# Twelve 2 KB buffers for nine, transposition chains begun at the end of their product, x split by halves of a chunk, and the first MLP product done two blocks at a time

## The chip, the cores and the metric

The kernel runs on one core of a Trainium2 chip. The metric is the device time of one execution in microseconds (us). The engines are TensorE (PE, matrix products, with its weight loads shown apart as PEld), VectorE (DVE), ScalarE (ACT), GpSimdE (POOL) and SyncE (SP), which here issues all transfers. Each engine takes its own instructions in the order of the program; semaphores order them across engines.

## The reference

One decoder layer in float32, for 256 tokens and a model width of 2048. Three branches (a gated delta rule "gdn", a forgetting attention "fox", a cross attention to 256 memory tokens) are projected, gated and summed; then an MLP of width 8192.

```python
h = rms_norm(x, g_mix)
proj = h @ w_in                       # qkv_a, z_a, ..., q_m, gates
kv_m = rms_norm(mem, g_mem) @ w_mem_kv
o_a, o_b, o_m = gdn(...), fox(...), cross(...)
y = gate_a * (o_a @ w_up_gdn) + gate_b * (o_b @ w_up_fox) + gate_m * (o_m @ w_up_mem)
x = x + y @ w_out
h2 = rms_norm(x, g_mlp)
x = x + square(relu(h2 @ w_ff1)) @ w_ff2
```

## The kernel before

Every product is made as three products of rounded halves: a weight is cast to its high part `whi` (ACT, L151), the rest `wlo` is weight less high part (DVE, L152), activations are held as high and low part too, and the low-low product is left out. Weights come in blocks of 1 MB through the SP queue (`wf`, 4 buffers, L159); a block is split in two halves, each into a `whi` and a `wlo` of 4 KB for each partition, of which there are 5 each. A half is worth 12 matmuls in `gemm_a` and 16 in `gemm_b`.

`gemm_a` (L162) has the activations as stationary side and 512 weight columns as moving side: for each of the 128 contraction rows and each half of the tokens the matmuls L176 (`whi`), L177 (`wlo`), L178 (`whi` with the low activations), into two accumulators. `gemm_b` (L191) has the weights as stationary side: for each k one matmul of 512 columns (`whi` with both halves of the activations, written H below) and one of 256 (`wlo`, written L), into one accumulator, one block of 128 outputs after another; at the last k the two change places. Then ACT copies the low half out (`lo`, L205) and DVE adds (L206). `gemm_b` makes q, k, v of the gdn branch and the first MLP product, FF1 (L946); everything else is `gemm_a`. There are 4 accumulators of 2 KB (`acc`) and 4 further PSUM tiles (`sm`).

The program is fully unrolled. Small work runs beside the products as generators: `spawn` (L127) puts one in a list, `tick` (L131) advances every one by a step after each weight block, `finish` runs one to its end. `prep_x` (L266 on) makes the row statistics, broadcasts them (`rbc`, L288) and splits x in four chunks, `key_T` and `query_T` norm the heads of a product (`sq`, `hnf`, `hn`) and turn them through memory (`ta`, `turn`, `tb`, then `kTm` or `qTm`). The stages are: keys and values of the memory (kv, up to about 100 us), queries to it (mq), gdn q/k/v and its chain, z, fox, the gates and up-products (`combine`, L835), the output product, then the MLP in four quarters, each FF1 then FF2 (`gemm_a`).

The order on each engine is made at build time by a list scheduler: an instruction takes its place when its inputs and its buffer are free by the scheduler's reckoning, in order of priority; transfers and splits of weights have a raised priority (`high_priority(PRI)`). Tiles of 4 KB come from pool `s4` (`t4`, N4 buffers), those of 2 KB from `s2p` (`t2`, N2 buffers, among them `gt`, `hn`, `ta`, `tb`, `lo`, `fr`).

Of the kernel before, what the change touches and what calls it, by code (L numbers as in the profile page):

```python
# [18 lines left out]
KT = D // P  # L19
# [10 lines left out]
K_ID, K_ONE, K_GMASK, K_FMASK, K_M32, K_TBD, K_PBD, K_EV, K_OD, K_RST = (  # L30
    0, 128, 256, 640, 1024, 1152, 1156, 1160, 1161, 1162)
NCST = K_RST + 256
N4, N2 = 23, 9
NWF, NHI, NLO = 4, 5, 5
XB = 3
PRI = 100
# [3 lines left out]
def body(ctx: ExitStack, tc: tile.TileContext, I, out, dbg=None):  # L40
# [57 lines left out]
    def acc():  # L98
        return pacc.tile([P, 512], F32, tag="acc", name=nm("acc"))
# [27 lines left out]
    def spawn(gen):  # L127
        bg.append(gen)
        return gen

    def tick():  # L131

        for g in list(bg):
            if next(g, 0) == 0:
                bg.remove(g)
# [55 lines left out]
    def gemm_b(srcs, act, dst):  # L191

        t = t2("lo")
        for f, src in enumerate(srcs):
            ps = acc()
            parts = weights(src)
            for k in range(KT):
                wh, wl = (t_[:, k % 8 * 128:k % 8 * 128 + 128] for t_ in parts[k // 8])
                ops = [(ps, wh, act.both(k)), (ps[:, 0:256], wl, act(k)[0])]
                if k == KT - 1:  # L200
                    ops.reverse()
                for i, (o, w, x) in enumerate(ops):
                    mm(o, w, x, start=(k == 0 and i == 0), stop=(k == KT - 1 and i == 1))  # L203
            tick()
            A.copy(t[:, f, :], ps[:, 256:512])  # L205
            V.tensor_tensor(dst[:, f, :], ps[:, 0:256], t[:, f, :], ALU.add)  # L206

    def turned(src, n=4):

# [14 lines left out]
    def load_T(src, q):  # L224
        xt = t4("xt")
        nc.sync.dma_start(xt, src[:, q * 4:q * 4 + 4, :])
        return xt

    def split_scaled(dst, xt, q, gcol, rows=None, ks=range(4)):

        for k in ks:
            g = pk[:, gcol + q * 4 + k:gcol + q * 4 + k + 1]
            h, l = dst(q * 4 + k)
            if rows is None:
                A.activation(h, xt[:, k, :], AF.Copy, scale=g)
                V.scalar_tensor_tensor(l, xt[:, k, :], g, h.bitcast(F32), ALU.mult, ALU.subtract)
            else:
                V.scalar_tensor_tensor(xt[:, k, :], xt[:, k, :], g, rows, ALU.mult, ALU.mult)
                A.copy(h, xt[:, k, :])
                V.tensor_tensor(l, xt[:, k, :], h.bitcast(F32), ALU.subtract)  # L240
# [34 lines left out]
    def prep_x():  # L275
        nc.sync.dma_start(cst, I["cst"])
        yield 1
        for _ in row_stats("m", I["mem"]):
            yield 1
        for _ in row_stats("x", I["x"]):  # L280
            yield 1

        pr = sm()
        for tb in range(2):
            dg = tp.tile([P, 128], F32, tag="dg", name=nm("dg"))
            V.tensor_scalar(dg, ident, rstd_x[:, tb:tb + 1], None, ALU.mult)
            mm(pr[:, tb * 128:tb * 128 + 128], ones, dg, start=True, stop=True)
        A.copy(rbc, pr[:, :256])  # L288
        yield 1
        for q in range(4):  # L290
            split_scaled(hact, load_T(I["xT"], q), q, C_GX, rbc)
            yield 1


    gq = cp.tile([P, 3], F32, name="gq")
# [29 lines left out]
    def key_T(ps, rs, nh, dh, dst, tb, gains):  # L325
        f2 = tp.tile([P, 4], F32, tag="hnf2", name=nm("hnf2"), bufs=4)[:, :nh]
        head_scale(ps, rs, nh, dh, f2)
        n = t2("hn", (P, 512))
        V.tensor_tensor(n.rearrange("p (h d) -> p h d", h=nh), ps.rearrange("p (h d) -> p h d", h=nh),
                        f2.unsqueeze(2).to_broadcast([P, nh, dh]), ALU.mult)  # L330
        yield 1
        yield from heads_T(n, dst, tb, gains)

    def query_T(ps, rs, nh, dh, dst, tb, gains, f2):

        head_scale(ps, rs, nh, dh, f2)
        yield from heads_T(ps, dst, tb, gains)
# [8 lines left out]
    bg_prep = spawn(prep_x())  # L346
    for g in range(2):
        def ev(tb, ps, g=g):
            spawn(key_T(ps, rstd_m[:, tb:tb + 1], 2, 256, kTm[g], tb,
                         [pk[:, C_MK + i:C_MK + i + 1] for i in range(2)]))  # L350
        gemm_a([I["w_kv"][g, c] for c in range(4)], mact, ev, first if g == 0 else None)
    for g in range(2):
        def ev(tb, ps, g=g):
# [376 lines left out]
    def fox_gemm(g):  # L730
        qT, kT, v = t4("qTf"), t4("kTf"), t4("vf", (P, 2, 512))
        fq = tp.tile([P, 2, 4], F32, tag="fqf", name=nm("fqf"))

        def ev_q(tb, ps):
            spawn(query_T(ps, None, 4, 128, qT, tb, [gq[:, 0:1]], fq[:, tb, :]))

        def ev_k(tb, ps):
            spawn(key_T(ps, None, 4, 128, kT, tb, [pk[:, C_FK:C_FK + 1]]))

        def ev_v(tb, ps):  # L740
            A.copy(v[:, tb, :], ps)
        for i, ev in enumerate((ev_q, ev_k, ev_v)):
            gemm_a([I["w_fox"][2 * i + g, c] for c in range(4)], hact, ev)
        return qT, kT, v, fq
# [67 lines left out]
    def y_T(tb, g):  # L812
        pt = turned(y[0](tb, g))
        yield 1
        yield 1
        t = slice(tb * 128, tb * 128 + 128)
        split(in_32(yT[0].h.t[g][:, :, t]), in_32(yT[0].l.t[g][:, :, t]), pt)
        yield 1

    def up(br, g, act, gt, last=False):  # L820
        def ev(tb, ps):
            ys = y[0](tb, g)
            if gt is None:
                V.tensor_tensor(ys, ps, ys, ALU.mult)
                return
            V.tensor_tensor(gt[tb], ps, gt[tb], ALU.mult)
            V.tensor_tensor(ys, ys, gt[tb], ALU.add)
            if last:
                next(spawn(y_T(tb, g)))
        gemm_a([I["w_up"][br, g, c] for c in range(2)], act, ev)  # L830

    def combine(br, act, last):
# [5 lines left out]

    for g in range(2):
        def ev(tb, ps, g=g):  # L840
            spawn(query_T(ps, None, 2, 256, qTm[g], tb, [gq[:, 1 + i:2 + i] for i in range(2)],
                          fqm[:, tb, 2 * g:2 * g + 2]))
        gemm_a([I["w_mq"][g, c] for c in range(4)], hact, ev)

    hs_gen = spawn(head_scalars())
# [54 lines left out]
    def x2_T(tb, g):  # L900
        xs = xcol(tb, g)
        if g < 3:
            pt = turned(xs)
            yield 1
            yield 1
            pts = [pt[:, c] for c in range(4)]
            wide = lambda ap: ap.rearrange("p (a r) -> p a r", a=4)
        else:
            pt = sm()
            for c in range(4):  # L910
                nc.tensor.transpose(pt[:, c * 128:c * 128 + 128], xs[:, c * 128:c * 128 + 128], ident)
            pts = [pt[:, c * 128:c * 128 + 128] for c in range(4)]
            wide = lambda ap: ap
        for c in range(4):
            k = g * 4 + c
            t = slice(tb * 128, tb * 128 + 128)
            gc = pk[:, C_GL + k:C_GL + k + 1]
            o_h, o_l = (wide(b_[:, t]) for b_ in h2(k))
            A.activation(o_h, pts[c], AF.Copy, scale=gc)
            V.scalar_tensor_tensor(o_l, pts[c], gc, o_h.bitcast(F32), ALU.mult, ALU.subtract)  # L920
        junk = t2("sq", (P, 512))
        A.activation(junk, xs, AF.Square, accum_out=s2[:, tb, g:g + 1])
        yield 1

    for g in range(4):
        def ev(tb, ps, g=g):
            xs = xcol(tb, g)
            V.tensor_tensor(xs, xs, ps, ALU.add)
            gen = spawn(x2_T(tb, g))
            if g < 3:  # L930
                next(gen)
        gemm_a([I["w_out"][g, c] for c in range(4)], yT[0], ev)
    tick()

# [7 lines left out]
    for q in range(4):  # L942
        u = Split("u", 16)
        for fp in range(8):
            r = t2("fr")
            gemm_b([I["w_ff1"][q * 16 + fp * 2 + i] for i in range(2)], h2, r)  # L946
            A.activation(r, r, AF.Relu)
            V.tensor_tensor(r, r, r, ALU.mult)
            sl = slice(fp * 2, fp * 2 + 2)
            split(u.h[sl], u.l[sl], r)  # L950
        for g in range(4):
            def ev(tb, ps, g=g):
                xs = xcol(tb, g)
                n = 256 if q == 3 and g == 3 else 512
                for i in range(0, 512, n):
                    V.scalar_tensor_tensor(xs[:, i:i + n], ps[:, i:i + n], r2[:, tb:tb + 1], xs[:, i:i + n],
                                           ALU.mult, ALU.add)
                    if q == 3:
                        nc.sync.dma_start(out[tb * 128:tb * 128 + 128, g * 512 + i:g * 512 + i + n], xs[:, i:i + n])
            gemm_a([I["w_ff2"][g, q * 4 + c] for c in range(4)], u, ev, final=(q == 3 and g == 3))  # L960
# [90 lines left out]
```

## Time and profile before

| what | value |
|---|---|
| median of 3 runs | 1741.11 us (1740.29 to 1741.96) |
| the profiled execution, its own time | 1741.53 us |
| its span in the trace | 1739.4 us |
| PE busy / weight loads | 1717.0 us (99%) / 1443.0 us |
| DVE, ACT, POOL busy | 1066.7, 847.5, 41.1 us |
| granted clock, mean | 0.998 |
| DMA | 354.29 MB, 204 GB/s on average |

Busy time is the sum of the records of an engine; for PE the ends are modelled, so a wait shorter than a pipeline's depth isn't seen in it, and the distance from start to start of two matmuls tells more. The span begins with the first and ends with the last instruction; what lies around it is 1741.53 - 1739.4 = 2.1 us.

### The profile page before, as it was taken

To read this page: it belongs to the slowest core of one execution; us is meant where nothing else is said; L and a number is where in the kernel's file an instruction comes from. 1 tells how busy PE (TensorE), PEld (TensorE's weight loads), DVE (VectorE), ACT (ScalarE), POOL (GpSimd) and SP (SyncE) were. 2 spreads that over 40 slices of the span, in tenths; PEclk is the share of its full clock that TensorE was granted. 3 is DMA by queue.
4 is the path that set the end of the run, shared out by engine and by line. 5 is a ranking of instruction groups with operands and counts; after the bars stand their busy time and mean duration, and the time that the engine had idled before them with its cause. 6 is when DMAs were issued, how large, how long until landed. Compare 5 with 4: busy or idle time off the path is not lost.

```text
span 1739.4 us, 21618 instructions
## 1 busy us (share of the span) xinstructions
PE 1717.0 (99%) x8356; PEld 1443.0 (83%) x8356; DVE 1066.7 (61%) x1453; ACT 847.5 (49%) x1138; POOL 41.1 (2%) x45
## 2 busy tenths in 40 slices
PE   8999999999999999899999999999999999999998
PEld 6878888888888888788888888888888888888887
DVE  5666777987755556555565666555665566555653
ACT  7554765435455344544444564534553355335532
POOL 0000001011000000000000000000000000000000
PEclk9999999999999999999999999999999999999999
DMA  9776555555646567555668765555555555555562
GB/s 379 235 279 215 190 197 170 194 176 187 214 158 231 193 215 248 182 174 193 218 223 282 244 202 187 194 193 194 181 184 193 193 194 179 198 194 182 191 205 85
DMA packets 89526, 354.29 MB, mean 204 GB/s; under 512 B 17984, under 2 KB 41168, under 8 KB 51664
## 3 DMA queue, kind: packets, MB, share of 16 engines
q1 hardware_dynamic: 89424, 352.92, 59.4%
q8 instruction: 65, 1.06, 0.2%
q14 instruction: 37, 0.30, 0.1%
HBM read 337.66 MB, written 15.22 MB: 203 GB/s over the span
## 4 chain that ended last, share of the span: by engine, by line
PE 95%; DMA 1%; DVE 1%; ACT 1%; issue 0%; SPq 0%; POOL 0%; DVEq 0%; ACTq 0%
PE acc L203 28%; PE acc L176 21%; PE acc L177 21%; PE acc L178 21%; DMA wf<-w_kv 1%; DVE wlo L152 1%; ACT whi L151 0%; DMA tb<-turn 0%; PE sm L366 0%; PE sm L588 0%; PE sm L391 0%; PE sm L535 0%; DMA turn<-ta 0%; PE sm L677 0%; PE sm L671 0%
## 5 line engine op out<-in xcount | busy, mean ns | idle before, releaser
L152 DVE TENSOR_TENSOR wlo<-wf,whi 128x1024 fp32r<-128x1024 f32 x594 | 723.7, 1222 | 575.4 <-ACT whi L151 567.2
L151 ACT CAST whi<-wf 128x1024 fp32r<-128x1024 f32 x594 | 622.5, 1051 | 764.7 <-PE acc L178 555.3
L203 PE MATMUL acc<-h,whi 128*128 128x512 f32 x1408 | 495.5, 400 | 1.5 <-DVE xp L206 1.5
L203 PE MATMUL acc<-h,wlo 128*128 128x256 f32 x1408 | 382.6, 282 | 0.0
L203 PEld LDWEIGHTS acc<-h,whi 128*128 128x128 f32 x1408 | 260.6, 189 | 58.7 <-issue 1.8
L176 PE MATMUL acc<-whi,h 128*128 128x512 f32 x704 | 278.1, 395 | 6.1 <-ACT gt L809 6.1
L177 PE MATMUL acc<-wlo,h 128*128 128x512 f32 x704 | 275.3, 391 | 0.2 <-DVE wlo L152 0.2
L178 PE MATMUL acc<-whi,h 128*128 128x512 f32 x704 | 275.2, 391 | 0.0
L203 PEld LDWEIGHTS acc<-h,wlo 128*128 128x128 f32 x1408 | 266.9, 190 | 8.2
L176 PE MATMUL acc<-whi,uh 128*128 128x512 f32 x512 | 199.3, 389 | 0.0
L178 PE MATMUL acc<-whi,ul 128*128 128x512 f32 x512 | 199.3, 389 | 0.0
L177 PE MATMUL acc<-wlo,uh 128*128 128x512 f32 x512 | 199.3, 389 | 0.0
L176 PEld LDWEIGHTS acc<-whi,h 128*128 128x128 f32 x704 | 132.7, 188 | 34.7 <-ACT gt L809 6.9
L178 PEld LDWEIGHTS acc<-whi,h 128*128 128x128 f32 x704 | 132.5, 188 | 27.9
L177 PEld LDWEIGHTS acc<-wlo,h 128*128 128x128 f32 x704 | 132.7, 189 | 27.4 <-DVE wlo L152 0.5
L177 PEld LDWEIGHTS acc<-wlo,uh 128*128 128x128 f32 x512 | 96.2, 188 | 20.1
L176 PEld LDWEIGHTS acc<-whi,uh 128*128 128x128 f32 x512 | 96.2, 188 | 19.8
L178 PEld LDWEIGHTS acc<-whi,ul 128*128 128x128 f32 x512 | 96.1, 188 | 19.8
L176 PE MATMUL acc<-whi,mh 128*128 128x512 f32 x128 | 50.3, 402 | 7.8 <-ACT whi L151 7.8
L177 PE MATMUL acc<-wlo,mh 128*128 128x512 f32 x128 | 51.5, 402 | 1.1 <-DVE wlo L152 1.1
L178 PE MATMUL acc<-whi,ml 128*128 128x512 f32 x128 | 50.8, 397 | 0.0
L178 PE MATMUL acc<-whi,yl 128*128 128x512 f32 x128 | 49.8, 390 | 0.0
(259 smaller groups left out, 1453.5 us busy)
## 6 DMA issues: line engine op xcount, KB each, us to landing
wf<-w_ff SPq DMA_DIRECT2D x128, 1024.0 KB, 4.8
wf<-w_gate SPq DMA_DIRECT2D x48, 1024.0 KB, 4.8
wf<-w_qkv SPq DMA_DIRECT2D x24, 1024.0 KB, 5.4
wf<-w_fox SPq DMA_DIRECT2D x24, 1024.0 KB, 4.8
wf<-w_up SPq DMA_DIRECT2D x24, 1024.0 KB, 4.9
wf<-w_out SPq DMA_DIRECT2D x16, 1024.0 KB, 5.4
wf<-w_kv SPq DMA_DIRECT2D x15, 1024.0 KB, 9.2
turn<-ta SPq DMA_DIRECT2D x42, 256.0 KB, 2.3
```

Source lines behind the costliest of these rows:

```text
L151: A.copy(hi, c)
L152: V.tensor_tensor(lo, c, hi.bitcast(F32), ALU.subtract)
L176: mm(ps[tb], xh[:, t], wh, start=(k == 0), stop=False)
L177: mm(ps[tb], xh[:, t], wl, start=False, stop=False)
L178: mm(ps[tb], xl[:, t], wh, start=False, stop=(k == nk - 1))
L203: mm(o, w, x, start=(k == 0 and i == 0), stop=(k == KT - 1 and i == 1))
```

## The change

1. The pool of 2 KB tiles has 12 buffers for 9, that of 4 KB tiles 22 for 23.
2. `spawn_now` spawns a generator and takes its first step at once; it is used for `key_T` and `query_T` after the kv, mq and fox products, whose first step ran at the next `tick` before.
3. `prep_x` splits a chunk of x in two steps of two k each, with a `yield` after each, where one step did four.
4. FF1 uses the new `gemm_b2`: two blocks of 128 outputs side by side, in two accumulators. For each k it issues both H, then both L (at the last k both L first); four weight halves are split at its start, `tick` runs every 8 k, and both evacuations stand at its end.

```diff
-N4, N2 = 23, 9
+N4, N2 = 22, 12
+    def spawn_now(gen):
+        next(spawn(gen))
+    def gemm_b2(srcs, act, dst):
+        t = t2("lo")
+        ps = [acc(), acc()]
+        with tc.high_priority(PRI):
+            w = [wtile(src.shape[1]) for src in srcs]
+            for w_, src in zip(w, srcs):
+                nc.sync.dma_start(w_, src)
+            halves = [[split_half(w_, i) for w_ in w] for i in range(2)]
+        for k in range(KT):
+            ops = []
+            for f in range(2):
+                wh, wl = (t_[:, k % 8 * 128:k % 8 * 128 + 128] for t_ in halves[k // 8][f])
+                ops.append((f, ps[f], wh, act.both(k)))
+                ops.append((f, ps[f][:, 0:256], wl, act(k)[0]))
+            ops = ops[0::2] + ops[1::2] if k < KT - 1 else ops[1::2] + ops[0::2]
+            for i, (f, o, w_, x) in enumerate(ops):
+                mm(o, w_, x, start=(k == 0 and i < 2), stop=(k == KT - 1 and i >= 2))
+            if k % 8 == 7:
+                tick()
+        for f in range(2):
+            A.copy(t[:, f, :], ps[f][:, 256:512])
+            V.tensor_tensor(dst[:, f, :], ps[f][:, 0:256], t[:, f, :], ALU.add)
         for q in range(4):
-            split_scaled(hact, load_T(I["xT"], q), q, C_GX, rbc)
-            yield 1
+            xt = load_T(I["xT"], q)
+            for i in range(2):
+                split_scaled(hact, xt, q, C_GX, rbc, ks=(2 * i, 2 * i + 1))
+                yield 1
-            spawn(key_T(ps, rstd_m[:, tb:tb + 1], 2, 256, kTm[g], tb,
+            spawn_now(key_T(ps, rstd_m[:, tb:tb + 1], 2, 256, kTm[g], tb,
...
-            spawn(query_T(ps, None, 2, 256, qTm[g], tb, [gq[:, 1 + i:2 + i] for i in range(2)],
+            spawn_now(query_T(ps, None, 2, 256, qTm[g], tb, [gq[:, 1 + i:2 + i] for i in range(2)],
...
-            gemm_b([I["w_ff1"][q * 16 + fp * 2 + i] for i in range(2)], h2, r)
+            gemm_b2([I["w_ff1"][q * 16 + fp * 2 + i] for i in range(2)], h2, r)
```

How this moves instructions, at three places. ACT in the kv stage, from the broadcast of the statistics (`rbc`) on, before: two casts of weights stand ahead of the scaled key copies (`kTm`) and the squares (`sq`).

```order
L288 COPY rbc<-sm_505 128x256
L151 CAST whi_589<-wf_587 128x1024
L151 CAST whi_593<-wf_587 128x1024
L323 ACTIVATE kTm_192<-tb_419,pk 128x2x128 x2
L306 ACTIVATE sq_569,hnf_568<-acc_312,rstd_m 128x256 x2
L306 ACTIVATE sq_579,hnf_578<-acc_313,rstd_m 128x256
L151 CAST whi_655<-wf_653 128x1024
```

And after:

```order
L316 COPY rbc<-sm_509 128x256
L353 ACTIVATE kTm_192<-tb_379,pk 128x2x128 x2
L336 ACTIVATE sq_519,hnf_518<-acc_332,rstd_m 128x256 x2
L336 ACTIVATE sq_529,hnf_528<-acc_333,rstd_m 128x256
L155 CAST whi_601<-wf_599 128x1024
L155 CAST whi_605<-wf_599 128x1024
L336 ACTIVATE sq_529,hnf_528<-acc_333,rstd_m 128x256
```

The casts of the same half of a block, the 18th, now stand behind the copies and three squares; on DVE its `wlo` stands behind the `hnf` and `hn` of the same chain, where it stood ahead of them.

ACT at the first gdn product, before, from the softmax of the memory attention (`Lm`) to the low copies (`lo`) of that product:

```order
L151 CAST whi_1612<-wf_1606 128x1024
L151 CAST whi_1681<-wf_1679 128x1024
L323 ACTIVATE qTm_896<-tb_1362,gq 128x2x128 x2
L151 CAST whi_1685<-wf_1679 128x1024
L375 ACT_TABLE_LOAD
L375 ACTIVATE Lm_1403,msv_1405<-sm_1398,mmx_1404,fqm 128x2x128 x2
L205 COPY lo_1308<-acc_1309 128x256
L205 COPY lo_1308<-acc_1416 128x256
```

And after:

```order
L405 ACT_TABLE_LOAD
L405 ACTIVATE Lm_1403,msv_1405<-sm_1398,mmx_1404,fqm 128x2x128 x2
L209 COPY lo_1338<-acc_1339 128x256
L155 CAST whi_1608<-wf_1606 128x1024
L209 COPY lo_1338<-acc_1416 128x256
L155 CAST whi_1612<-wf_1606 128x1024
L353 ACTIVATE qTm_896<-tb_1241,gq 128x2x128 x2
L155 CAST whi_1681<-wf_1679 128x1024
```

The softmax and the copy that frees the first accumulator moved ahead of four casts.

ACT at the evacuation of one gate product (`gt`), in the kernel after; the kernel before has the same rows in the same order, under its own line numbers (L151, L809, L785):

```order
L155 CAST whi_6322<-wf_6320 128x1024
L155 CAST whi_6326<-wf_6320 128x1024
L155 CAST whi_6356<-wf_6354 128x1024
L839 ACT_TABLE_LOAD
L839 ACTIVATE gt_6001<-acc_6003 128x512
L839 ACTIVATE gt_6002<-acc_6004 128x512
L815 COPY pTf_6267<-tb_6181 128x384
```

Nothing moved here: `gt` stands behind the same casts as before.

## Rows read from the trace of the kernel before

**Rows 1.** The page, chain that ended last, share of the span by engine.
```profile
PE 95%; DMA 1%; DVE 1%; ACT 1%; issue 0%; SPq 0%; POOL 0%; DVEq 0%; ACTq 0%
```

**Rows 2.** Waits of PE: who waited for whom, us in total, times, longest.
```profile
PE acc L176 <- ACT gt L809: 6.1, 2, 3.0
PE acc L177 <- DVE wlo L152: 1.2, 3, 0.5
```

**Rows 3.** Timeline of ACT, 695 to 699 us: start, us, instruction, idle before.
```profile
695.84 1.04 ACT L151 CAST whi<-wf 128x1024 fp32r<-128x1024 f32 x1 [1.66 <-PE acc L178]
696.90 1.28 ACT L809 ACT_TABLE_LOAD   x1
698.20 1.09 ACT L809 ACTIVATE gt<-acc 128x512 f32<-128x512 f32 x2
```

**Rows 4.** Timeline of PE in the same stretch.
```profile
695.19 0.39 PE L177 MATMUL acc<-wlo,oMh 128*128 128x512 f32 x1
695.42 0.39 PE L178 MATMUL acc<-whi,oMl 128*128 128x512 f32 x1
698.85 0.50 PE L176 MATMUL acc<-whi,h 128*128 128x512 f32 x1 [3.04 <-ACT gt L809]
```

**Rows 5.** Busy time by stretch with granted clock (PEclk), behind that wait.
```profile
698.00:702.00 4.00, 3.15 (x10) 2.55 (x11) 2.64 (x5) 1.67 (x4) 0.00 (x0) 0.76 0.39 164
702.00:706.00 4.00, 4.00 (x16) 3.17 (x15) 1.23 (x1) 1.46 (x2) 0.00 (x0) 0.81 0.00 0
```

**Rows 6.** Timeline of ACT, kv stage, 56 to 64 us.
```profile
56.71 0.37 ACT L288 COPY rbc<-sm 128x256 f32<-128x256 f32 x1 [7.05 <-PE sm L287]
56.98 2.00 ACT L151 CAST whi<-wf 128x1024 fp32r<-128x1024 f32 x2
58.88 0.90 ACT L323 ACTIVATE kTm<-tb,pk 128x256 f32<-128x256 f32 x2
...
61.03 2.00 ACT L151 CAST whi<-wf 128x1024 fp32r<-128x1024 f32 x2
```

**Rows 7.** Timeline of DVE in the same stretch.
```profile
60.73 0.17 DVE L311 TENSOR_SCALAR hnf<-hnf 128x2 f32<-128x2 f32 x1 [0.30 <-ACT sq L306]
...
62.65 2.35 DVE L152 TENSOR_TENSOR wlo<-wf,whi 128x1024 fp32r<-128x1024 f32 x2
```

**Rows 8.** Timeline of PE, kv stage, three places.
```profile
60.41 0.39 PE L176 MATMUL acc<-whi,mh 128*128 128x512 f32 x1
...
71.07 0.39 PE L178 MATMUL acc<-whi,ml 128*128 128x512 f32 x1
...
73.06 0.40 PE L178 MATMUL acc<-whi,ml 128*128 128x512 f32 x1
...
88.52 0.39 PE L178 MATMUL acc<-whi,ml 128*128 128x512 f32 x1
...
90.70 0.39 PE L178 MATMUL acc<-whi,ml 128*128 128x512 f32 x1
```

**Rows 9.** Timeline of PE at the second gdn product, 178 to 181 us.
```profile
178.80 0.40 PE L203 MATMUL acc<-h,whi 128*128 128x512 f32 x1
180.73 0.47 PE L203 MATMUL acc<-h,whi 128*128 128x512 f32 x1 [1.52 <-DVE xp L206]
```

**Rows 10.** Timeline of PE in FF1, at the border of two blocks.
```profile
1041.24 0.40 PE L203 MATMUL acc<-h,wlo 128*128 128x256 f32 x2
1041.48 0.63 PE L203 MATMUL acc<-h,whi 128*128 128x512 f32 x2
1041.94 0.28 PE L203 MATMUL acc<-h,wlo 128*128 128x256 f32 x1
```

**Rows 11.** Timeline of PE in FF1, inside a block.
```profile
1100.00 0.40 PE L203 MATMUL acc<-h,whi 128*128 128x512 f32 x1
...
1102.12 0.40 PE L203 MATMUL acc<-h,whi 128*128 128x512 f32 x1
```

**Rows 12.** Chain of work in order of time, FF1 of the second quarter: start, us, what.
```profile
1202.41 90.45 PE acc L203 x512
```

More of the change, by code (lines that the diff above doesn't have):

```diff
@@ L348, in ev @@
         def ev(tb, ps, g=g):
-            spawn(key_T(ps, rstd_m[:, tb:tb + 1], 2, 256, kTm[g], tb,
-                         [pk[:, C_MK + i:C_MK + i + 1] for i in range(2)]))
+            spawn_now(key_T(ps, rstd_m[:, tb:tb + 1], 2, 256, kTm[g], tb,
+                            [pk[:, C_MK + i:C_MK + i + 1] for i in range(2)]))
         gemm_a([I["w_kv"][g, c] for c in range(4)], mact, ev, first if g == 0 else None)
@@ L734, in ev_q @@
         def ev_q(tb, ps):
-            spawn(query_T(ps, None, 4, 128, qT, tb, [gq[:, 0:1]], fq[:, tb, :]))
+            spawn_now(query_T(ps, None, 4, 128, qT, tb, [gq[:, 0:1]], fq[:, tb, :]))
         def ev_k(tb, ps):
-            spawn(key_T(ps, None, 4, 128, kT, tb, [pk[:, C_FK:C_FK + 1]]))
+            spawn_now(key_T(ps, None, 4, 128, kT, tb, [pk[:, C_FK:C_FK + 1]]))
         def ev_v(tb, ps):
@@ L828, in ev @@
             if last:
-                next(spawn(y_T(tb, g)))
+                spawn_now(y_T(tb, g))
         gemm_a([I["w_up"][br, g, c] for c in range(2)], act, ev)
@@ L840, in ev @@
         def ev(tb, ps, g=g):
-            spawn(query_T(ps, None, 2, 256, qTm[g], tb, [gq[:, 1 + i:2 + i] for i in range(2)],
-                          fqm[:, tb, 2 * g:2 * g + 2]))
+            spawn_now(query_T(ps, None, 2, 256, qTm[g], tb, [gq[:, 1 + i:2 + i] for i in range(2)],
+                              fqm[:, tb, 2 * g:2 * g + 2]))
         gemm_a([I["w_mq"][g, c] for c in range(4)], hact, ev)
@@ L928, in ev @@
             V.tensor_tensor(xs, xs, ps, ALU.add)
-            gen = spawn(x2_T(tb, g))
-            if g < 3:
-                next(gen)
+            (spawn_now if g < 3 else spawn)(x2_T(tb, g))
         gemm_a([I["w_out"][g, c] for c in range(4)], yT[0], ev)
```

## The prediction

> **What bounds the kernel now.** I read the chain that ended last first: 95% of the span is PE's own work [rows 1], so only two things can move the time: a wait of PE, or the pace at which PE takes its matmuls. The list of PE's waits comes next [rows 2]: the largest behind the start is the evacuation of a gate product, `gt`, twice, 6.1 us in all; the short ones are for `wlo`, in the kv stage. Then the timelines of ACT and DVE around each wait, to see what stands ahead of the releaser in its queue. Last come the steps of PE from start to start, since a busy PE is not one at its peak: in `gemm_a` a step is 0.23 us [rows 4]; in FF1 a pair of H and L takes 90.45 / 256 = 0.353 us [rows 12].
>
> **The buffers and the gate waits: 0.** At 695 us ACT's cast had to wait for PE's last matmul to let go of a `whi` buffer (idle 1.66 us, released by PE); it ended at 696.88, a table load of 1.28 us followed, then `gt`, and only its first half, done at 698.8, let PE go on [rows 3]. PE stood from 695.42 to 698.85, 3.43 us where a step is 0.23, so 3.2 us were lost [rows 4]. There are two such waits [rows 2], 6.4 us together. Behind the one at 695 the granted clock shows 0.76 and 0.81 of full speed over two stretches of 4 us [rows 5]: (0.24 + 0.19) x 4 = 1.7 us more. So these two places hold 8.1 us, the largest sum that is to be had. The new buffers are of the 2 KB pool, to which `gt` belongs; but what the cast waits for is a `whi` buffer, of which there are five in both kernels, and the order on ACT around `gt` is the same in both, cast by cast. The wait is made by that order: `gt` behind a cast that waits for PE, PE behind `gt`. I take 0 and keep -8.1 as a rival.
>
> The Trainium skill (Perfetto Trace Analysis, "Identifying Performance Opportunities") says that the same gap repeating on the engine that should be saturated can mean that there isn't enough SBUF or PSUM for the next tile, that is, too few buffers. By that rule, with the pool that grows being the one that lacks, the sum would be 8.1 us lower than mine. The trace agrees that a buffer is waited for [rows 3], but it is one of a pool that the change leaves alone.
>
> **Chains at once and x by halves (kv stage): -0.1 us.** Two of the waits for `wlo` stand in a row of late casts: from 71.07 to 73.06 PE made four steps in 1.99 us and from 88.52 to 90.70 four in 2.18 us [rows 8], where 4 x 0.23 = 0.92 is due; 1.1 and 1.3 us, 2.4 in all, are lost. In the first, the splits of a whole chunk of x stood on DVE and ACT between casts. The changed order has four more casts ahead of the first split of x, and at most two k of x between casts, so I expect both to go: -2.4.
>
> The same edit makes a new wait. The 18th half is due on PE at 60.41 [rows 8]. Before, its cast ran at 56.98, right behind `rbc` [rows 6]. Now two `kTm` copies and three `sq` stand ahead, which took from 58.88 to 61.03, 2.15 us, and PE makes `rbc`'s product four matmuls later, 4 x 0.23 = 0.9 us. So the cast begins at 56.98 + 0.9 + 2.15 = 60.0 and, with 1.0 each, its `whi` is there at 61.0: 0.6 us late. On DVE the `wlo` now stands behind `hnf`, the step of POOL and `hn`: from the first `hnf` to the `wlo` went 62.65 - 60.73 = 1.92 us, and one `wlo` takes 1.18 [rows 7]. With the squares done at 60.0 this is 60.0 + 1.92 + 1.18 = 63.1, while PE, after its first two matmuls, asks for it at 61.0 + 0.46 = 61.5: 1.6 more. Together 2.2 to 2.3 us. Bounds: 0, if the scheduler's order hides a free `whi` that I missed, and 2.3; I take 2.3 since the queues run in order. Net -0.1, bounds -2.4 and +2.3 (the old waits staying). Who waits for this: PE alone, and all later halves shift with it, which gives the casts slack.
>
> The load of x goes through SP as four transfers as before, the weights' order on SP changes by a place or two; each half of a block lasts at least 12 x 0.23 = 2.8 us on PE against 1.0 of cast and 1.18 of `wlo`, so I cost that at 0. For mq the chain begins earlier too. It moves one `wlo` ahead of the small decay rows that PE's transposes near 164 us need; that is up to +1.2, and as those rows have fewer chain steps ahead of them, also down to -1.2. I take 0. For fox the same first step runs a few matmuls earlier, where PE has no listed wait [rows 2]: 0, with 1 us to each side.
>
> **The first gdn evacuation: -1.7 us.** From 178.80 to 180.73 PE made one step in 1.93 us, of which 1.52 are put down to `xp` [rows 9]; a step behind an H is about 0.24 there, so 1.7 us are lost. On ACT a cast, the table load and the two softmax rows stood ahead of the copy that `xp` needs. In the changed order that softmax and the copy stand ahead of four casts, so the accumulator is free some ten us before it is asked for. What would be late next is the second copy, behind one cast more, and it has a block of 16 pairs, 5.65 us, of cover. Bounds -1.7 and 0.
>
> **FF1 two blocks side by side: +1 us.** The work is the same: as many H, L and weight loads. What changes is the order H L H L to H H L L, for 4 x 8 x 16 = 512 groups of four. The rows show the new neighbours at the border of two blocks, where the last k is reversed: L L from 1041.24 to 1041.48, 0.24, and H H from there to 1041.94, 0.46 [rows 10]: 0.70 for four, against 2 x 0.353 = 0.707 [rows 12]. But inside a block six pairs take 2.12 us, 0.353 each [rows 11], and with the 16 borders in it the piece of 90.45 us gives the same 0.353 [rows 12], so a border neither gains nor costs. Rows are read to 0.01 us, so a group of four is known to about -0.01 to +0.01, or -5 to +5 us in all; as an L must now cover the load of a weight in 0.12 us that an H of 0.23 covered, I choose the positive side, 0.002 a group, +1. Twice the time between evacuations costs nothing as long as two of the four accumulators are free at a pair's end: a pair lasts 11.3 us and the two copies, adds and the casts ahead of them are 2 to 3 us.
>
> The Trainium skill (TensorE: Matmul & The Clock Gate, "Back-to-back issue gap") gives 216 ns between matmuls of 512 columns as an isolated gap, N / 2.4 + 2.5; an estimate by it for 256 columns is 109 ns, and 650 ns for the four in any order. By it FF1 would lose 29 us if the new order got rid of whatever keeps the pairs apart. The trace disagrees so far: two H in a row took 0.23 each, as 512 columns do in `gemm_a` [rows 4, 10].
>
> **Sum.** 0 - 0.1 - 1.7 + 1 = -0.8, on the profiled execution's 1741.53: 1740.7. That execution lay 0.4 over the median of 1741.11, so the median I predict is 1740.3 us. What a measurement here can tell from no change is 0.2%, 3.5 us.
>
> **Rivals.**
> - *Pace gain in FF1.* Two H in a row go as in `gemm_a`, 0.23 each, and two L in 0.24 [rows 4, 10]: 0.70 for four, 0.007 less than two pairs, x 512 = -3.6 instead of +1: 1735.7; with the reading error of 0.01 on it, down to 1730.6. For it: the one border shown reads 0.70. Against: the piece with 16 borders shows no gain [rows 12]. Chance 0.13.
> - *The gate waits go.* 8.1 us less than my sum: 1732.2. Against: the unchanged order on ACT. Chance 0.06.
> - *Pace loss in FF1, slower.* Each L behind an L, and each H behind the second, is held by its weight load, since an L lasts only 0.12 us; at 0.01 each, 0.02 a group, x 512 = +10 instead of +1: 1749.5; at 0.01 a group 1744.4. It decides over the sign from 0.008 a group on (+4.2 us). For it: 0.12 for each L is what an H beside it leaves of a pair, 0.353 - 0.23, so nothing is gained there and the load's cover is halved. Against: again the piece of 90.45. Chance 0.15.
> - *The change doesn't do what it says:* the kv waits move but don't shrink, and the gdn copy still comes late. Then only FF1's +1 and 2 us of the new kv wait are left: 1744. Chance 0.08, still within 0.2%.
> - My forecast: chance 0.58, its own range 1737 to 1744.
>
> **How the numbers follow.** Faster by over 0.2% (under 1737.6): the two first rivals, 0.19, and 0.02 of the forecast's lower edge: 0.21. Slower by over 0.2% (over 1744.6): 0.15 and 0.01: 0.16. Within: 0.63. For 8 in 10, the range takes the forecast, the idle change and the near halves of the two FF1 rivals: 1733.5 to 1746.
>
> **What would show it.** In the changed kernel's trace: the same two waits for `gt`, 3.0 us each, the first at about 695 us, and a clock below 0.85 behind it; a new wait near 61 us for `whi` and `wlo`, about 2 us; none for `xp` near 179; pieces of FF1 of about 90.7 us for 512 matmuls. I am wrong if a piece of FF1 is outside 90.0 to 91.5, if the `gt` waits are gone, or if a wait appears that no row here names.

## The result, and the profile after

The changed kernel takes 1758.76 us (median of 4 runs, 1755.43 to 1760.48) against 1740.7 us (4 runs): the ratio is 1.0102, 95% interval 1.0089 to 1.0115, so it is slower by 18 us. The profiled execution took 1755.43 us with a span of 1753.7 us. Forecast were 1740.3 us and a range of 1733.5 to 1746.

The list of PE's waits answers to [rows 2] (engine and line, who is waited for, us in total, times, longest):

```profile
PE sm L666 <- issue: 11.5, 1, 11.5
PE acc L180 <- ACT whi L155: 8.6, 2, 8.0
PE acc L180 <- ACT gt L839: 6.1, 2, 3.0
PE acc L180 <- ACT zt L900: 2.6, 1, 2.6
PE sm L502 <- DVE ct L485: 1.6, 1, 1.6
PE acc L181 <- DVE wlo L156: 1.0, 1, 1.0
```

The two waits for `gt` stand as before. The largest wait is new and in a place that the prediction doesn't speak of: line 666, a small product of the gdn chain (L636 before). "issue" says that the profile shows no releaser. The timeline of PE there:

```profile
385.61 0.39 PE L182 MATMUL acc<-whi,h 128*128 128x512 f32 x1
397.53 3.59 PE L666 MATMUL sm<-Tc,Ms 128*128 128x32 f32 x16 [11.54 <-issue]
403.72 0.79 PE L180 MATMUL acc<-whi,h 128*128 128x512 f32 x1 [2.60 <-ACT zt L900]
```

And by stretches (busy time of PE, PEld, DVE, ACT, POOL, then the granted clock):

```profile
386.00:398.00 12.00, 0.47 (x3) 0.50 (x3) 11.17 (x32) 1.04 (x1) 0.00 (x0) 0.60 0.25 87
398.00:402.00 4.00, 3.12 (x15) 2.99 (x14) 1.64 (x4) 0.37 (x1) 0.00 (x0) 0.50 0.00 0
402.00:406.00 4.00, 2.28 (x8) 1.99 (x8) 2.52 (x6) 1.08 (x2) 0.00 (x0) 0.50 0.14 33
406.00:410.00 4.00, 4.00 (x17) 3.71 (x17) 1.30 (x3) 0.00 (x0) 1.09 (x2) 0.50 0.00 0
410.00:414.00 4.00, 4.00 (x18) 2.73 (x17) 0.61 (x2) 0.79 (x2) 0.00 (x0) 0.73 0.00 0
```

PE stands for 11.5 us, and behind that the clock is at half (1.2 GHz of 2.4) until some 412 us. So 11.5 us of wait, 2.6 us of a second one for `zt`, and up to (0.5 + 0.5 + 0.5 + 0.27) x 4 = 7 us of slow clock over the four stretches from 398 on make about 21 us.

What DVE did meanwhile tells why. Timeline of DVE at the end of the wait:

```profile
396.23 0.21 DVE L647 TENSOR_TENSOR X<-X,Xt 32x60 f32<-32x60 f32 x1
396.48 0.18 DVE L645 TENSOR_TENSOR Xt<-Mu,X 32x31 f32<-32x31 f32 x1
396.69 0.48 DVE L621 SCALAR_TENSOR_TENSOR Ata<-sm,sc,Ea 128x256 f32<-128x256 f32 x1
397.09 0.34 DVE L621 SCALAR_TENSOR_TENSOR Atb<-sm,sc,Eb 128x128 f32<-128x128 f32 x1
```

In the kernel before, the same evacuations stand ahead of the long series on `X`:

```profile
362.23 0.48 DVE L591 SCALAR_TENSOR_TENSOR Ata<-sm,sc,Ea 128x256 f32<-128x256 f32 x1
...
370.16 0.17 DVE L615 TENSOR_TENSOR Xt<-Mu,X 32x31 f32<-32x31 f32 x1
```

The products whose results go to `Ata` and `Atb` hold PSUM tiles of the kind `sm`, of which there are four. There are four such products, and PE had done the last of them long before:

```profile
357.93 0.60 PE L618 MATMUL sm<-qT,kT 128*128 128x256 f32 x2
```

So no `sm` tile is free for line 666 from then on. The first is let go at 397.4, when the first pair of evacuations ends, and PE goes on at 397.53. The evacuation itself comes right behind the last row that reads `Mu`. `Ata` and `Mu` are both tiles of the 4 KB pool, which has 22 buffers now for 23. This is a reading so far; the runs below test it.

The second wait, for `zt`, seems to have the same root. `zt` is a 4 KB tile too, and on ACT its row starts 0.03 us after the last evacuation into `Ata` ends (402.56 + 0.48 = 403.04):

```profile
403.07 1.08 ACT L900 ACTIVATE zt<-acc 128x512 f32<-128x512 f32 x2 [1.54 <-DVE Ata L621]
```

The first MLP product, which answers to [rows 12], from the chain in order of time:

```profile
1220.25 89.31 PE acc L229 x512
```

It is 1.14 us shorter than before, and so are the others: 4.6 us gained.

### The profile page after: what moved, and what is told of

It is laid out like the page before. It is cut to its first block, busy times and chain, and to the rows that moved or that the text cites. A ratio compares the mean times of both kernels' runs of the same rounds, so it can differ in the third digit from the quotient of the medians.

```text
span 1753.7 us, 21604 instructions
## 1 busy us (share of the span) xinstructions
PE 1717.9 (98%) x8356; PEld 1446.0 (82%) x8356; DVE 1060.4 (60%) x1453; ACT 844.6 (48%) x1138; POOL 40.6 (2%) x45
## 4 chain that ended last, share of the span: by engine, by line
PE 93%; DMA 3%; DVE 1%; issue 1%; SPq 1%; ACT 1%; POOL 0%; DVEq 0%; ACTq 0%; POOLq 0%
PE acc L229 20%; PE acc L180 20%; PE acc L182 20%; PE acc L181 20%; PE acc L207 7%; DMA xs<-mem 1%; DMA wf<-w_kv 1%; DMA turn<-ta 1%; DVE wlo L156 1%; DMA tb<-turn 1%; PE sm L421 0%; PE sm L618 0%; PE sm L565 0%; PE sm L666 0%; PE sm L396 0%
## 5 line engine op out<-in xcount | busy, mean ns | idle before, releaser
L229 PE MATMUL acc<-h,whi 128*128 128x512 f32 x1024 | 317.2, 395 | 0.0
L229 PEld LDWEIGHTS acc<-h,wlo 128*128 128x128 f32 x1024 | 187.9, 188 | 42.4
L229 PE MATMUL acc<-h,wlo 128*128 128x256 f32 x1024 | 196.8, 279 | 0.0
L229 PEld LDWEIGHTS acc<-h,whi 128*128 128x128 f32 x1024 | 158.5, 189 | 2.8
L207 PE MATMUL acc<-h,whi 128*128 128x512 f32 x384 | 138.1, 403 | 0.0
L207 PE MATMUL acc<-h,wlo 128*128 128x256 f32 x384 | 104.7, 283 | 0.0
L207 PEld LDWEIGHTS acc<-h,whi 128*128 128x128 f32 x384 | 71.9, 189 | 14.9
L207 PEld LDWEIGHTS acc<-h,wlo 128*128 128x128 f32 x384 | 73.0, 190 | 1.8
```

Source lines behind the costliest of these rows:

```text
L229: mm(o, w_, x, start=(k == 0 and i < 2), stop=(k == KT - 1 and i >= 2))
```

## The experiments

Each run is compared with runs of the kernel before on the same chip; their medians were 1739.23, 1738.94 and 1739.23 us in the three groups (e1 to e4, e5 to e8, and the rest).

**The pools.** The theory: with 22 buffers `Ata` of the second gdn chain has none until `Mu` is dead. The rival: the chains begun at once, or the halves of x, bring the series on `X` ahead of it.

First the changed kernel with the old pools:

```diff
-N4, N2 = 22, 12
+N4, N2 = 23, 9
```

> The changed kernel with the pools as before (23 of 4 KB, 9 of 2 KB). Theory one (the 4 KB buffer given up leaves the second gdn chain's Ata tile without a buffer until its X chain on DVE has read Mu for the last time; PE stands 11.5 us and then runs at half clock): no long wait near 386 us, FF1 pieces of 89.3 us, time about 1735 us. Rival (the chains begun at once or the halves of x bring the X chain ahead of the evacuations of Ata): the wait stays and the time stays at 1755 to 1760 us.

Measured: 1736.0 us, ratio 0.9979 (0.997 to 0.9988). No wait at L666 is left.

Then the kernel before with the new pools:

```diff
-N4, N2 = 23, 9
+N4, N2 = 22, 12
```

> The kernel before with the new pools alone (22 of 4 KB, 12 of 2 KB). Theory one: the wait of PE of some 11 us near 390 us appears here too, time 1740.7 + 19 = about 1760 us. Rival: no such wait, about 1741 us.

Measured: 1761.13 us, ratio 1.0123 (1.0106 to 1.0139). PE's waits in it:

```profile
PE sm L636 <- issue: 11.1, 1, 11.1
PE acc L176 <- ACT zt L870: 2.6, 1, 2.6
```

The half clock lasts longer here, to 420 us:

```profile
416.00:420.00 4.00, 4.00 (x15) 3.39 (x15) 1.92 (x2) 0.00 (x0) 0.00 (x0) 0.50 0.13 18
420.00:424.00 4.00, 4.00 (x24) 3.49 (x23) 2.34 (x5) 2.13 (x3) 0.88 (x1) 0.99 0.66 264
```

The pools alone make the whole loss, 21.9 us; without them the changed kernel is faster than before. The rival falls.

And the changed kernel with the lost 4 KB buffer back at equal memory:

```diff
-N4, N2 = 22, 12
+N4, N2 = 23, 10
```

> The changed kernel with 23 buffers of 4 KB and 10 of 2 KB, the same memory as 22 and 12. Theory one: no long wait near 386 us, as with 23 and 9: about 1735 us. If the number of 2 KB buffers matters beside it (more tiles let the chains run further ahead), it differs from 23 and 9 by a us or more.

Measured: 1736.09 us, ratio 0.9978 (0.9969 to 0.9988), the same as with 9. The memory is that of 22 and 12, so it is the one 4 KB buffer that matters, and a tenth 2 KB buffer brings nothing.

That `Mu` holds the buffer was tested by moving that tile, at 22 and 12, to the other pool:

```diff
-        Mu = t4("Mu", (NU, 32, 32))
-        nc.sync.dma_start(Mu, dM.rearrange("t h (b j) i -> (t h b) j i", b=4))
+        Mus = [t2("Mu", (NU, 16, 32)) for _ in range(2)]
+        for i in range(2):
+            nc.sync.dma_start(Mus[i], dM.rearrange("t h (b j) i -> (t h b) j i", b=4)[:, i * 16:i * 16 + 16, :])
...
-            V.tensor_tensor(t, Mu[:, j, j + 1:32].unsqueeze(2).to_broadcast([NU, n, j + 1]),
+            V.tensor_tensor(t, Mus[j // 16][:, j % 16, j + 1:32].unsqueeze(2).to_broadcast([NU, n, j + 1]),
```

> The changed kernel, pools 22 and 12, but the tile Mu of the gdn chain in two tiles of 2 KB for one of 4 KB. If it is Mu that holds the buffer on which Ata waits, a 4 KB buffer is free now and the wait of 11.5 us near 386 us is gone: about 1735.5 us. If the wait comes from something else that 22 buffers bring, it stays: 1755 to 1760 us.

Measured: 1734.83 us, ratio 0.9973 (0.9962 to 0.9983); the long wait and the one for `zt` are gone, as in the two runs with 23. So the 4 KB pool lacks one buffer at that time, and two of the new 2 KB ones pay for it. That the buffer is handed from `Mu` to `Ata` rests on the order of the rows above (`Ata` 0.03 us behind the last reader of `Mu`): any 4 KB tile fewer at that time would have given the same run.

**FF1 by pairs.** First the part alone (with `gemm_b2` as in the change):

```diff
-            gemm_b([I["w_ff1"][q * 16 + fp * 2 + i] for i in range(2)], h2, r)
+            gemm_b2([I["w_ff1"][q * 16 + fp * 2 + i] for i in range(2)], h2, r)
```

> The kernel before with the first MLP product done two blocks at a time, nothing else. If the gain of 1.14 us for each of the four FF1 pieces (90.45 to 89.31) belongs to the order of the matmuls alone: 1740.7 - 4.6 = 1736.1 us, with everything ahead of the MLP as before. If it needs the other parts: about 1741 us.

Measured: 1734.65 us, ratio 0.9976 (0.9966 to 0.9985), with pieces of 89.31 us. Is it the two accumulators, or the grouping of H with H and L with L? Two accumulators without the grouping:

```diff
-            ops = ops[0::2] + ops[1::2] if k < KT - 1 else ops[1::2] + ops[0::2]
+            if k == KT - 1:
+                ops = [ops[1], ops[0], ops[3], ops[2]]
...
```

> FF1 two blocks at a time as in the run with that part alone, but in the order H L of the one block, H L of the other. If the gain comes from grouping H with H and L with L: pieces of FF1 of 90.45 us again and about 1739 us. If it comes from changing between two accumulators: 89.3 us and about 1734.7 us.

Measured: 1738.57 us, ratio 0.9993 (0.9983 to 1.0003): no gain from two accumulators, nor from the rest of `gemm_b2`, which this run has too. Then grouping in one accumulator, two k at a time, and eight k at a time, in `gemm_b` as a whole (gdn q, k, v and FF1); the diff is that of two k, in the other run 8 stands for each 2:

```diff
-            for k in range(KT):
+            for k0 in range(0, KT, 2):
+                hs, ls = [], []
+                for k in range(k0, k0 + 2):
...
+                    hs.append((ps, wh, act.both(k)))
+                    ls.append((ps[:, 0:256], wl, act(k)[0]))
+                ops = hs + ls if k0 + 2 < KT else ls + hs
...
```

> The kernel before with gemm_b in groups of two k within one block and one accumulator: H H L L (gdn q, k, v and FF1). If grouping alone gives the gain: FF1 pieces of 89.3 us, and 24 blocks of gdn by 0.07 us each, 1.7 us more: 1739.2 - 4.6 - 1.7 = about 1733 us. If it takes two accumulators: 90.45 us and 1739 us.

> As the run before, in groups of eight k: eight H, then eight L. If the gain goes with the number of changes between H and L (half of them gone gave 4.4 ns for each pair, so 7 of 8 give 7.8 ns): FF1 pieces of 88.45 us, 1739.2 - 8 - 3 = about 1728 us. If an L must cover the weight load of the next one (0.120 us by the steps at a block's border, against 0.117): no further gain, or a loss of up to 0.003 x 1400 = 4 us.

Measured: 1735.66 us (0.9973, 0.9961 to 0.9985) and 1734.29 us (0.9973, 0.9961 to 0.9985). The same FF1 piece in the chains of the three, H L H L in two accumulators, groups of two k, groups of eight k:

```profile
1199.65 90.40 PE acc L226 x512
```

```profile
1199.15 89.47 PE acc L205 x512
```

```profile
1200.16 89.07 PE acc L205 x512
```

It is the grouping, and one accumulator is enough for it. The timeline of the changed kernel shows a group of four at 0.70 us (from 1250.08 to 1250.78) where two pairs took 0.707 [rows 12]:

```profile
1250.08 0.63 PE L229 MATMUL acc<-h,whi 128*128 128x512 f32 x2
1250.55 0.39 PE L229 MATMUL acc<-h,wlo 128*128 128x256 f32 x2
1250.78 0.62 PE L229 MATMUL acc<-h,whi 128*128 128x512 f32 x2
```

With eight, sixteen L (two runs of eight that meet at the reversed end) take 1.91 us, 0.119 each:

```profile
1251.91 2.08 PE L205 MATMUL acc<-h,wlo 128*128 128x256 f32 x16
1253.82 2.46 PE L205 MATMUL acc<-h,whi 128*128 128x512 f32 x10
```

So a pair costs 89.07 / 256 = 0.348 us, of which L takes 0.119 and H the other 0.229: H behind H goes at `gemm_a`'s pace of 0.23 [rows 4], and a change between the two costs the H a few ns, while L is no faster. From two k to eight the gain is 0.4 us a piece, not the 1.0 that the expectation drew from the number of changes. The extra 1.7 to 3 us expected from the gdn products don't show in the medians (4.65 us in all; in FF1 alone three pieces gain 1.38 each, and the first, from the start of its first matmul to that of its last, 0.8: 4.9). In the run with eight k the wait for `xp` has grown from 1.5 to 2.2 us, which takes back a part; the rest is left open.

**The other two parts.** The chains begun at once (the same edit for the fox and mq products), and the halves of x:

```diff
-            spawn(key_T(ps, rstd_m[:, tb:tb + 1], 2, 256, kTm[g], tb,
+            spawn_now(key_T(ps, rstd_m[:, tb:tb + 1], 2, 256, kTm[g], tb,
...
```

> The kernel before with the chains of the kv, fox and mq products begun at once, nothing else. My prediction had a new wait near 61 us of 2.3 us against old ones of 2.4, and 1.7 us less at the first gdn product: 1737.5 us. If the halves of x are what moves the kv casts: about 1739 us.

Measured: 1742.86 us, ratio 1.0017 (1.0007 to 1.0027). Its waits:

```profile
PE acc L180 <- ACT whi L155: 8.9, 2, 8.3
PE sm L476 <- DVE ct L459: 1.6, 1, 1.6
PE acc L181 <- DVE wlo L156: 1.6, 2, 1.0
```

The wait for `xp`, 1.5 before, is gone, as forecast. That for `wlo` has grown from the 1.2 of [rows 2], the second one for `whi` from 0.2 to 0.6 (8.9 less the 8.3 at the start), and that for `ct`, 0.7 and 0.5 before, is 1.6 in one. Together that is 3.8 us against 4.1 before, so the listed waits don't make the 3.6 us. The granted clock differs. Behind the wait for `ct` and behind the second wait for `gt`, first before, then here:

```profile
168.00:172.00 4.00, 4.00 (x17) 3.44 (x16) 1.86 (x4) 1.05 (x1) 0.70 (x1) 0.62 0.70 206
172.00:176.00 4.00, 4.00 (x25) 3.50 (x24) 2.92 (x4) 1.86 (x3) 0.00 (x0) 1.00 0.93 320
740.00:744.00 4.00, 4.00 (x19) 3.31 (x18) 2.31 (x4) 1.49 (x3) 0.00 (x0) 1.00 0.02 4
```

```profile
168.00:172.00 4.00, 4.00 (x14) 3.15 (x15) 2.52 (x7) 0.00 (x0) 0.00 (x0) 0.50 0.72 293
172.00:176.00 4.00, 4.00 (x17) 3.44 (x17) 1.56 (x2) 1.85 (x3) 0.00 (x0) 0.67 0.56 166
740.00:744.00 4.00, 3.59 (x10) 2.90 (x11) 2.49 (x4) 1.25 (x3) 0.00 (x0) 0.66 0.29 121
```

That is up to 0.38 x 4 = 1.5 us before against (0.5 + 0.33 + 0.34) x 4 = 4.7 here. It fits the ten executions: nine have a mean clock of 0.996 or 0.997, and the tenth, with 0.998 as in 15 of the 18 executions of the kernel before, took 1738.68 us. So the 3.6 us are mostly clock. The clock behind `gt` is low in some executions and not in others, with the same wait ahead of it; what decides is not shown.

```diff
-            split_scaled(hact, load_T(I["xT"], q), q, C_GX, rbc)
-            yield 1
+            xt = load_T(I["xT"], q)
+            for i in range(2):
+                split_scaled(hact, xt, q, C_GX, rbc, ks=(2 * i, 2 * i + 1))
+                yield 1
```

> The kernel before with x split by halves of a chunk, nothing else. If this alone removes the waits for wlo near 71 and 89 us: 1739 - 2 = 1737 us. Otherwise about 1739 us.

Measured: 1739.33 us, ratio 0.9997 (0.9988 to 1.0007). Its list of waits has no `wlo` left, yet the median is unchanged. There was less to gain than the 2.4 us of [rows 8]: six other runs with the kv stage of the kernel before (e2, e6, e6b, e7, e8, e13) list one wait for `wlo`, that near 71 us, and none near 89:

```profile
PE acc L177 <- DVE wlo L152: 0.5, 1, 0.5
```

By [rows 8] the place near 71 us holds 1.1 us, which the interval of the median (-2.1 to +1.2 us) can't tell from nothing.

**The gate waits.** They were 8.1 us in the prediction's account, and twelve buffers in the shared pool did nothing for them. Here `gt` gets two buffers that nothing else uses:

```diff
-N4, N2 = 23, 9
+N4, N2 = 23, 8
...
-            gt = [t2("gt", (P, 512)) for _ in range(2)]
+            gt = [tp.tile([P, 512], F32, tag="gtt", name=nm("gt"), bufs=2) for _ in range(2)]
```

> The kernel before with the two gt tiles of a gate product in two 2 KB buffers of their own, and 8 for 9 in the 2 KB pool. If the two waits of PE for gt come from the 2 KB pool handing gt a buffer that a fox tile still holds (so that ACT's order puts gt behind the casts): both waits of 3.0 us and the stretch of lower clock behind the first go, 1739 - 8 = about 1731 us. If they come from the priority of the casts: they stay, 1739 us.

Measured: 1729.79 us, ratio 0.9941 (0.9923 to 0.9958). No wait for `gt` is in its list, and on ACT the first `gt` of the fox stage stands at 682.7, 15 us earlier than in [rows 3]:

```profile
681.43 1.28 ACT L809 ACT_TABLE_LOAD   x1
682.72 0.60 ACT L809 ACTIVATE gt<-acc 128x512 f32<-128x512 f32 x1
```

So the wait came from where `gt` gets its buffer: in the shared 2 KB pool the order puts it behind the casts, with buffers of its own it doesn't. Which tile held a buffer, and why three more in the shared pool didn't reach `gt`, isn't shown. The shared pool is also one buffer smaller here, and no run has 8 with `gt` among them; with 9, 10 and 12 the two waits were 6.1 us together.

**The parts that help, together:** `gemm_b` in groups of eight k, `gt` in its own buffers, and the gate evacuation in a `high_priority(2 * PRI)` block, on the kernel before with 23 and 8.

```diff
+            with tc.high_priority(2 * PRI):
+                A.activation(dst(tb), ps, AF.Sigmoid)
```

> The kernel before with gemm_b in groups of eight k, the gt tiles in two buffers of their own (8 in the 2 KB pool) and the gate evacuation at a raised priority. If the two gains are independent: 1739 - 4.5 - 8 = about 1726.5 us. If the smaller pool brings back a wait elsewhere: 1730 us or more.

Measured: 1725.46 us, ratio 0.9922 (0.9905 to 0.994): 13.8 us less than before, the fastest of all. The two gains add up (4.65 and 9.44 make 14.1). The raised priority was not run by itself; the sum leaves no gain for it.

## Why the prediction was wrong

- **The pools: the step that failed.** The part on "the buffers and the gate waits" weighed only the three buffers that come, not the one that goes. Where the change gives up the 23rd buffer of 4 KB it was costed at nothing without a word on who uses that pool. It cost 21.9 us (e2), all of the loss: 11.1 of wait, 2.6 of a second wait, and the rest in the 22 us of half clock from 398 to 420. The list of waits [rows 2] couldn't show it, as a buffer that is there makes no wait; what shows it is the order on DVE in the kernel after, in which the rows for `Ata` stand behind the series on `X`. The prediction looked at the order in the kv stage, at the first gdn product and at the gates; the gdn chain has no term in it.
- **The gate waits stay: right, for a wrong reason.** They stayed at 6.1 us. But the reason given, that the buffer waited for is a `whi` of another pool, doesn't hold: two 2 KB buffers set apart remove both waits (e6b). The cast's wait for `whi` is what ACT's rows show; that `gt` stands behind it hangs on the 2 KB pool. The rule of the Trainium skill (Perfetto Trace Analysis, "Identifying Performance Opportunities"), that repeated gaps can mean too few buffers, was the better guide; these runs add that more buffers in a shared pool needn't reach the tile that lacks one. The gain of 9.4 us bears out the price of 8.1 within the run-to-run spread.
- **FF1: the size and the sign were off.** +1 was taken, about -4.6 came (e3, pieces of 89.31 us); the first rival, -3.6, was near. The border of two blocks had read 0.70 for a group of four [rows 10], and that is what every group takes now. I set it aside because a piece with 16 borders showed no gain [rows 12]; but 16 x 0.007 is 0.1 us in 90.45, and the pair inside a block, read from 2.12 us over six [rows 11], is uncertain by 0.01 / 6, or 0.4 us in 256 pairs. The average could not speak against the row. The slower rival, the weight load behind a short L, is not what decides: L behind L takes 0.119.
- **The kv stage: the mechanism was right.** The new wait came at the 18th half: PE lost 0.73 at `whi` and 1.3 at `wlo`, 2.0 together, where 2.3 was worked out. The rows, to be read beside [rows 8]:

```profile
59.83 0.39 PE L182 MATMUL acc<-whi,ml 128*128 128x512 f32 x1
60.79 0.73 PE L180 MATMUL acc<-whi,mh 128*128 128x512 f32 x2 [0.58 <-ACT whi L155]
62.57 0.50 PE L181 MATMUL acc<-wlo,mh 128*128 128x512 f32 x1 [1.05 <-DVE wlo L156]
```

  From 59.83 to 60.79 is one step of 0.23 and 0.73 lost, from 60.79 to 62.57 two steps and 1.3. The old waits at 71 and 89 us are gone. Against the profiled execution, which had both, the net is near the -0.1 forecast; in executions with the one at 71 us alone only 1.1 is saved against the 2.0, so the net is nearer +1.
- **The first gdn evacuation: right in its place, given back in the clock.** The 1.5 us wait for `xp` is gone. The waits for `ct` went from 1.2 in two to 1.6 in one, within the bounds of -1.2 to +1.2 that the prediction put on mq and costed at 0. What it had no term for is the lower clock behind that wait, up to 3.3 us in e11 against 1.5 before. With the chains begun at once alone the kernel is 3.6 us slower (interval 1.2 to 4.7), and beside FF1 and the halves of x the two parts together cost about 1.3 (e1 against e3, with intervals that overlap), so the forecast of -1.8 for these two parts was 3 to 5 us too low.
- **The sum of the parts:** 21.9 - 4.6 + 3.6 + 0.1 = 21.0 against the 18.1 measured; the difference is about what the chains cost less beside the other parts.

## What to carry to other kernels

A pool that gives up a buffer must be costed like an added wait: ask which tile takes the last buffer at its fullest time, and look in the new order for an evacuation that moved behind a long series, since the old trace can't show it. Here a tile on which PE waits was better served by buffers of its own than by a larger shared pool. Try grouping matmuls of one size (1.0 to 1.4 us for 512 matmuls here), and trust a row that shows the new order once over an average that can't resolve it. Cost a wait of PE with the clock behind it: in e11 the waits for `ct` grew by 0.4 us and the slow clock behind them by up to 1.8.

## What the runs showed of the hardware

Matmuls of 512 and 256 columns that take turns cost 0.353 us a pair; in groups of two 0.349 (89.31 / 256), in groups of eight 0.348. The short ones don't get faster in a row (0.119 each); the long ones do, to 0.229. And the 11.5 us in which PE stood were followed by about 14 us at half clock in the kernel after, and the 11.1 us of e2 by 22. In that time PE did small matmuls, waited once more and took up `gemm_a` again. In e2 the whole came to 21.9 us, about twice the wait.
